# Gates of output block 1 as seven-product steps, x sums split ahead of block 0's gates, down weights and gated sums in another order

## The chip, the cores and the metric

The kernel runs on one core of a Trainium2 chip. The metric is the device time of one execution in microseconds. TensorE (PE) multiplies, VectorE (DVE), ScalarE (ACT) and GpSimd (POOL) do the elementwise work, and SyncE (SP) issues most transfers.

## The reference, cut to what matters

One layer over 512 positions with a model width of 1024, all in float32:

```
h = rms_norm(x);  proj = h @ w_in                  # conv B | conv C | conv in | q | k | v | f | gates
y_conv = (cb * causal_dwconv3(cc * cin)) @ w_out_conv
o = forgetting_attention(q, k, v, log_sigmoid(f))  # 8 heads of 64
y_attn = o @ w_out_attn
g_conv, g_attn = split(sigmoid(g_logit + b_gate))  # 2 x 1024 columns
x = x + (g_conv * y_conv + g_attn * y_attn) @ w_o
h = rms_norm(x)
a, b = split(causal_dwconv3(h @ w_up))             # 2 x 2816 columns
x = x + (silu(a) * b) @ w_down
return rms_norm(x)
```

## The kernel before

Everything is kept transposed: features on the 128 partitions, the 512 positions along a row. Every float32 operand of a product is split into a high part (rounded to the format TensorE multiplies quickly) and a low part (the rest), and a product is three passes: high x high, low x high, high x low. ScalarE makes the high part of a weight tile (wh, L275), VectorE the low part by a subtraction (wl, L279). Weights stream through `raw` tiles, fetched some tiles ahead; `stream` is the fixed list of weight tiles, and `split()` makes the parts of the next one.

Stages in order: the projections and, between them, attention; then the mixer, output block by output block (`for j in range(KB)`, eight blocks of 128 features): the two gates of block j, the tile `mix{j}` which makes yc and ya, and the merge m = gate_A * yc + gate_B * ya, split into mh and ml; then w_o; then the channel mixer in two phases of hidden pairs j = 0..11 and 12..21: up products (`up{2j}`, `up{2j+1}`), the taps of the convolution, silu and product (`glu`), and at the end of each phase the down products of that phase.

Part of the products goes by a seven-product scheme (`seven`) on 2 x 2 arrangements of blocks: two output blocks, two inner blocks, two halves of the positions. Seven products of 256 positions stand in for eight, and need sums of operands. Weight sums, called forms, are added up in DRAM by transfers (`make_forms`: SyncE's `put`, GpSimd's `add`), one group of forms per two steps. The sums of x are made on VectorE (`x_sums`), split by `x_split(q)` into xth and xtl for four quarters q. A step has a P tile (three products of a pair of blocks, 18 matmuls for two pairs) and an F tile (four products, 24 matmuls). In `passes` all high passes of a tile come first, two for each product, then the passes with the low part of the weight.

Work that has no fixed place is put in the list `later` with a due count of splits, a cost in microseconds and tags. `run_later`, called in each `split`, takes from it what fits; `flush` and `flush_only(tags)` force it out at once. Instructions that are recorded through `keep` hold the order in which the program is written; the others are placed by a scheduler after the last split.

GJ is the first block whose gates go by seven products: blocks 0 and 1 go directly before (two times 48 matmuls each, block 0's already at the end of the projections), blocks 2 to 7 by steps P0, F0, P1, F1 and so on. SUP lists the hidden pairs whose up products go by seven products: 1, 2 and 5 in phase 0, 14 and 16 in phase 1. `glu` puts sums of the gated products (ge, go) into `later`: t13 and t24 (L1253 to L1258), and their splits `hl` into gh and gl (L1262, L1263).

Of the kernel before, what the change touches and what calls it, by code (L numbers as in the profile page):

```python
# [16 lines left out]
KB = D // P  # L17
# [25 lines left out]
PHASES = ((0, 12), (12, NP))  # L43
# [8 lines left out]
    + (((1, 6),), ((1, 7), (1, 8)), ((1, 9), (1, 10))),  # L52
)

GJ = 2
GATES = tuple(((j, q), (j, q + 1)) for j in range(GJ, KB) for q in (0, 2))

PLAIN = [(m, k) for m in (6, 7) for k in range(*PHASES[1])]
# [2 lines left out]
SUP = ((1, 2, 5), (14, 16))  # L61
# [9 lines left out]
def block_kernel(ctx, tc, xT, vecs, wv, win, wmix, wo, wup, wst, wdp, outT):  # L71
# [3 lines left out]
    nc = tc.nc  # L75
# [6 lines left out]
    def keep(ins):  # L82
        return tc.keep_in_program_order(ins)
# [17 lines left out]
    def col(i):  # L101
        return vec[:, i : i + 1]
# [22 lines left out]
    stream = [(f"v{kb}", wv[kb], S + H) for kb in range(KB)]  # L125
# [7 lines left out]
    for j in range(KB):  # L133
        if j >= GJ:
            stream += step_chunks(n) + step_chunks(n + 1)
# [5 lines left out]
    ff0 = len(stream)  # L141
# [14 lines left out]
    later = []  # L156
# [7 lines left out]
        return st  # L164

    def tag_of(k):
        return "raw" if stream[k][0][0] != "F" else "rf" if k >= ff0 else "rg"

    def load(upto):
        for k in range(len(raws), min(upto, len(stream) - 1) + 1):  # L170
            nm, src, ncol = stream[k]
            tag = tag_of(k)
            if held[tag] == NRAW[tag] or tag not in pools:
                return
            held[tag] += 1
            raw = pools[tag].tile([P, D], F32, tag=tag, name=f"raw_{nm}", bufs=NRAW[tag])
            if k == 0:

                keep(nc.scalar.dma_start(raw[:, VB:ncol], src[:, VB:]))
                keep(nc.sync.dma_start(raw[:, :VB], src[:, :VB]))  # L180
            else:
                keep(nc.sync.dma_start(raw[:, :ncol], src if tag == "raw" else made[src]))
            raws.append(raw[:, :ncol])


# [2 lines left out]
    made, todo_bg = {}, []  # L188
# [58 lines left out]
    def flush_only(tags):  # L247

        while n := [n for n, w in enumerate(later) if set(w[2]) & set(tags)]:
            with after_split():  # L250
                later.pop(n[0])[3]()
# [421 lines left out]
    def run_all(fs):  # L673
        for f in fs:
            f()
# [8 lines left out]
    for t in range(NT):  # L684
        src = pa[t][:, 4 * HD : VW].unsqueeze(1).to_broadcast([P, 4, H])
# [4 lines left out]
    z, e, o = (ap.tile([n, S], F32, tag="pp", name=nm, bufs=NPP) for nm in ("fz", "fe", "fo"))  # L690
# [82 lines left out]
    k = len(parts) + 2  # L773
# [21 lines left out]
    for i in range(n + LA):  # L795
# [8 lines left out]
        if 0 <= i - LA < n:  # L804
            pr, e, qb = units[i - LA]
# [60 lines left out]
    xm = xp.tile([P, KB, S], F32, tag="x1", name="xm")  # L866
# [14 lines left out]

    def mt(name):
        mt.n += 1
        return xm[:, (mt.n + 3) % KB, :]

    mt.n = 0

    def evac_gate(idx, dst):
        def f(p):
            g = mt(f"g{idx}")  # L890
            nc.vector.tensor_mul(g, p, rb1)
            nc.scalar.activation(g, g, AF.Sigmoid, bias=col(BG + idx))
            dst.append(g)

        return f
# [10 lines left out]
    k = [c[0] for c in stream].index("mix0")  # L906
# [52 lines left out]
    for j in range(KB):  # L959
        gs = []  # L960
        for _ in range(3):
            slot()
        if j == KB - 1:
            assert mt.n == 3 * KB
            x1 = xm
            nc.gpsimd.dma_start(x1[:, :4, :], xT[:, :4, :])
        if j == 0:
            evac_gate(0, gs)(gp[0])
            evac_gate(8, gs)(gp[1])
        elif j < GJ:  # L970
            run_all(proj(20 + j, f"ga{j}", evac_gate(j, gs), acc))
            run_all(proj(28 + j, f"gb{j}", evac_gate(8 + j, gs), acc))
        else:
            if j == GJ:
                acc = ring(3, 4, 2, 7)
            seven(GATES[2 * (j - GJ) : 2 * (j - GJ) + 2], 2 * (j - GJ), {j: (0, 1, 5, 6)}, gate_form, done=gate_pair(j, gs))
        wh, wl = chunk(f"mix{j}")
        yc, ya = acc(f"yc{j}"), acc(f"ya{j}")
        for pp, hh, ll, o in ((yc, ych, ycl, 0), (ya, oth, otl, 4)):
            for k in range(4):  # L980
                ks = slice((o + k) * P, (o + k + 1) * P)
                mm3(pp, wh[:, ks], wl[:, ks], hh[:, k, :], ll[:, k, :], k == 0, k == 3)
        if j >= GJ:
            split_next()
            flush()
        a, b = gs
        nc.vector.tensor_mul(a, a, yc)
        nc.vector.tensor_mul(b, b, ya)
        nc.gpsimd.tensor_add(a, a, b)
        nc.scalar.activation(mh[:, j, :], a, AF.Copy)  # L990
        nc.vector.tensor_sub(ml[:, j, :], a, mh.bitcast(F32)[:, j, :])
# [149 lines left out]
    def up(j, ph, rb2, pu=None):  # L1141
        uu = []

        def tap(i, z):
            u = fp.tile([P, S], F32, tag="fu", name=f"fu{j}{i}", bufs=3)
            taps(u, z, CF + 3 * (2 * j + i))
            uu.append(u)

        if j in SUP[ph]:
            c = 2 * SUP[ph].index(j)  # L1150
            slot()
            seven(
                UPD[ph][c : c + 2], NU[ph] + c, {j: USETS[j]}, lambda q, g: up_form(ph, q, g), of="x",
                done=lambda i, banks, ids: merge(ph, j, banks, ids, rb2, tap, uu),
            )
            slot()
            return
        evacs = []
        for i in range(2):
            slot()  # L1160
            p = pu[i] if pu else block(f"up{2 * j + i}", x1h, x1l, True)
            if i and j + 1 == PHASES[ph][1]:
                split_next()
                if any(("e",) in w[2] for w in later):
                    flush_only((("e",),))
                    split()
            z = [None]

            def mul(i=i, p=p, z=z):
                z[0] = fp.tile([P, S], F32, tag="fz", name=f"fz{j}{i}", bufs=4)  # L1170
                nc.vector.tensor_mul(z[0], p, rb2)

            evac = [(0.7, mul), (1.4, lambda i=i, z=z: tap(i, z[0]))]
            if i:
                evac.append((0, lambda: glu(ph, j, uu)))
            if any(("e",) in w[2] for w in later):
                later.extend((0, us, (("e",), acc.last) if x == 0 else (("e",),), f) for x, (us, f) in enumerate(evac))
            else:
                for _, f in evac:
                    f()  # L1180
# [46 lines left out]
    def glu(ph, j, uu):  # L1227
        a, b = uu
        q, k = j // 2, len(parts) - 1
        g0 = place(ph, q)  # L1230
        nc.scalar.activation(a, a, AF.Silu)
        if j == NP - 1:
            nc.scalar.activation(tbl, a[: 4 * H, :1], AF.Sqrt, scale=0.0, bias=eps[: 4 * H])
        if j % 2 == 0:
            ge = glu.even = fp.tile([P, 2, 2 * P], F32, tag="ge", name=f"ge{q}", bufs=2)
            keep(nc.gpsimd.tensor_mul(ge, a.rearrange(halves_of, h=2), b.rearrange(halves_of, h=2)))  # L1236
            return
        flush_only([("q", x) for x in range(q)])
        ge = glu.even
        go = fp.tile([P, 6, 2 * P], F32, tag="gr", name=f"go{q}")  # L1240

        def mul(eng):
            return eng.tensor_mul(go[:, 0:2, :], a.rearrange(halves_of, h=2), b.rearrange(halves_of, h=2))

        if j + 1 < PHASES[ph][1]:
            keep(mul(nc.gpsimd))
        else:
            later.append((k + 3, 0.7, (("q", q),), lambda: mul(nc.vector)))
        b11, b12 = ge[:, 0, :], ge[:, 1, :]
        b21, b22, t1, t2, t3, t4 = (go[:, i, :] for i in range(6))  # L1250

        def t13():
            nc.vector.tensor_sub(t1, b11, b12)  # L1253
            nc.vector.tensor_sub(t3, b22, b12)

        def t24():
            nc.vector.scalar_tensor_tensor(t2, t1, -1.0, b22, op0=ALU.mult, op1=ALU.subtract)
            nc.vector.scalar_tensor_tensor(t4, t2, -1.0, b21, op0=ALU.mult, op1=ALU.subtract)  # L1258

        def hl(src, gs):  # L1260
            def f():
                nc.scalar.activation(gh[:, gs, :], src, AF.Copy)  # L1262
                nc.vector.tensor_sub(gl[:, gs, :], src, gh.bitcast(F32)[:, gs, :])  # L1263

            return f


        d = (2, 3, 4) if j + 1 < PHASES[ph][1] else (4, 5, 6)
        w = [(d[0], 0.85, t13), (d[0], 0.85, t24), (d[1], 0.7, hl(ge[:, : 1 + ph, :], slice(g0, g0 + 1 + NF * ph, NF)))]
        w += [(d[x > 0 and 2 or 1], 0.7, hl(go[:, x : x + 2, :], slice(g0 + 1 + x, g0 + 3 + x))) for x in (0, 4, 2)]  # L1270
        at = next((x for x, i in enumerate(later) if ("e",) in i[2]), len(later))
        later[at:at] = [(k + n, us, (("q", q),), f) for n, us, f in w]
# [264 lines left out]
```

## Time and profile before

| | |
|---|---|
| median of three runs | 694.92 us (694.84 to 695.49) |
| profiled execution | 694.18 us |
| its span | 692.4 us |
| granted TensorE clock, mean | 0.997 |
| TensorE busy | 683.1 us (99%), 5936 matmuls |
| VectorE busy | 554.2 us (80%) |
| ScalarE busy | 368.3 us (53%) |
| GpSimd busy | 190.5 us (28%) |

A row of a timeline has the start, the duration, the engine, the line, the operation, the tiles (buffer numbers left out) and, in brackets, how long the engine stood idle ahead of it and what ended that. A row of several equal instructions has their count. Times of rows are from the start of the span. In a table of windows the count behind PE's busy time is that of the matmuls that touch the window.

### The profile page before, as it was taken

Reading aid. Unit: us, or ns where it says so; the run is one execution under the profiler, and the core shown is the slowest. Engines: PE = TensorE matmul, PEld = TensorE weight load, DVE = VectorE, ACT = ScalarE, POOL = GpSimd, SP = SyncE. Lnnn points to the kernel's source line nnn. Section 1 sums busy time; section 2 is a strip of 40 time slices with the busy share of each in tenths; the row PEclk is TensorE's granted clock in tenths of the full one; section 3 lists DMA queues with packets and bytes.
Section 4 is the critical chain, followed back from the end, with each engine's and each line's share of the span. In section 5 each row is a group of like instructions: output and inputs, shape, how many; then the busy total and the mean of one; then the engine's idle time right before and its main releaser. Section 6 shows DMA issues by size and latency. Waiting matters only on the chain. (4 is left out here: it accounts for less than half of the span.)

```text
span 692.4 us, 14690 instructions
## 1 busy us (share of the span) xinstructions
PE 683.1 (99%) x5936; PEld 680.6 (98%) x5936; DVE 554.2 (80%) x858; ACT 368.3 (53%) x579; POOL 190.5 (28%) x201
## 2 busy tenths in 40 slices
PE   9999999999999999999999999999999999999996
PEld 9999999999999999999999999999999999999995
DVE  6677787877578778769879699998787899988894
ACT  5675755554554444546554555545444544545572
POOL 6134947542020201214400144340100325231000
PEclk9999999999999999999999999999999999999998
DMA  8629999552568586788998498888945996676413
GB/s 308 225 67 293 216 243 204 134 120 92 185 144 221 166 268 205 230 308 213 158 313 241 126 233 222 200 242 231 252 149 167 337 231 157 188 168 182 154 31 122
DMA packets 65012, 137.53 MB, mean 199 GB/s; under 512 B 5760, under 2 KB 30352, under 8 KB 64688
## 3 DMA queue, kind: packets, MB, share of 16 engines
q1 hardware_dynamic: 44664, 107.28, 47.2%
q0 software_dynamic: 18464, 26.03, 23.4%
q10 hardware_dynamic: 1816, 3.29, 1.3%
q8 instruction: 46, 0.75, 0.4%
q14 instruction: 22, 0.18, 0.1%
HBM read 132.31 MB, written 47.71 MB: 260 GB/s over the span
## 5 line engine op out<-in xcount | busy, mean ns | idle before, releaser
L211 POOL DMA_DIRECT2D f<-in_wst_dram x66 | 77.7, 1371 | 27.1 <-DMA f<-f 26.8
L309 PE MATMUL p_up<-x1h,wh_up 128*128 128x256 f32 x416 | 81.2, 276 | 0.0
L309 PE MATMUL p_up<-x1l,wh_up 128*128 128x256 f32 x416 | 81.0, 276 | 0.0
L309 PE MATMUL p_up<-x1h,wl_up 128*128 128x256 f32 x416 | 81.0, 276 | 0.0
L279 DVE TENSOR_TENSOR wl_F<-raw_F,wh_F 128x1024 fp32r<-128x1024 f32 (+1 forms) x42 | 55.9, 1330 | 20.0 <-ACT wh_F L275 20.0
L275 ACT ACTIVATE wh_F<-raw_F 128x1024 fp32r<-128x1024 f32 (+1 forms) x42 | 44.3, 1054 | 39.5 <-PE dn L327 28.7
L309 PEld LDWEIGHTS p_up<-x1h,wh_up 128*128 128x128 f32 x416 | 62.7, 188 | 0.0
L309 PEld LDWEIGHTS p_up<-x1l,wh_up 128*128 128x128 f32 x416 | 62.7, 188 | 0.0
L309 PEld LDWEIGHTS p_up<-x1h,wl_up 128*128 128x128 f32 x416 | 62.6, 188 | 0.0
L309 PE MATMUL p_in<-xgh,wh_in 128*128 128x256 f32 x288 | 56.8, 279 | 0.0
L309 PE MATMUL p_in<-xgh,wl_in 128*128 128x256 f32 x288 | 56.6, 278 | 0.0
L309 PE MATMUL p_in<-xgl,wh_in 128*128 128x256 f32 x288 | 56.5, 278 | 0.0
L279 DVE TENSOR_TENSOR wl_P<-raw_P,wh_P 128x768 fp32r<-128x768 f32 (+1 forms) x42 | 41.7, 992 | 14.7 <-ACT wh_P L275 8.6
L327 PE MATMUL dn<-gh,wh_F 128*128 128x256 f32 x216 | 51.2, 277 | 1.2 <-ACT wh_F L275 1.2
L275 ACT ACTIVATE wh_P<-raw_P 128x768 fp32r<-128x768 f32 (+1 forms) x42 | 35.1, 835 | 32.1 <-PE dn L327 23.2
L327 PE MATMUL dn<-gl,wh_F 128*128 128x256 f32 x216 | 51.0, 276 | 0.0
L1236 POOL TENSOR_TENSOR ge<-fu,fu 128x512 f32<-128x512 f32 x11 | 20.1, 1831 | 110.5 <-DVE fu L570 85.6
L279 DVE TENSOR_TENSOR wl_up<-raw_up,wh_up 128x1024 fp32r<-128x1024 f32 x34 | 43.8, 1288 | 7.4 <-ACT wh_up L275 7.4
L275 ACT ACTIVATE wh_up<-raw_up 128x1024 fp32r<-128x1024 f32 x34 | 35.8, 1054 | 19.4 <-PE p_up L309 9.3
L309 PEld LDWEIGHTS p_in<-xgh,wh_in 128*128 128x128 f32 x288 | 44.7, 188 | 0.7
L309 PEld LDWEIGHTS p_in<-xgl,wh_in 128*128 128x128 f32 x288 | 43.7, 188 | 0.0
L309 PEld LDWEIGHTS p_in<-xgh,wl_in 128*128 128x128 f32 x288 | 43.6, 188 | 0.0
(343 smaller groups left out, 2211.8 us busy)
## 6 DMA issues: line engine op xcount, KB each, us to landing
raw_F<-f SPq DMA_DIRECT2D x41, 512.0 KB, 5.7
raw_up<-in_wup_dram SPq DMA_DIRECT2D x34, 512.0 KB, 5.6
raw_P<-in_wst_dram SPq DMA_DIRECT2D x41, 384.0 KB, 5.4
raw_in<-in_win_dram SPq DMA_DIRECT2D x24, 512.0 KB, 3.6
f<-in_wst_dram POOLq DMA_DIRECT2D x41, 256.0 KB, 6.8
f<-in_wst_dram SPq DMA_DIRECT2D x20, 512.0 KB, 7.1
f<-in_wst_dram POOLq DMA_DIRECT2D x20, 512.0 KB, 9.1
f<-f SPq DMA_DIRECT2D x40, 256.0 KB, 6.5
```

Source lines behind the costliest of these rows:

```text
L211: return lambda: keep(nc.gpsimd.dma_start(dst, src, accum_op=ALU.add))
L275: ins = nc.scalar.activation(hi, raw, AF.Copy)
L279: ins = nc.vector.tensor_sub(lo, raw, hi.bitcast(F32))
L309: keep(nc.tensor.matmul(out[:, cs], w, x[:, cs], start=start and i == 0 and c == 0, stop=stop and i == 2 and c == len(cut) - 1,))
L327: keep(nc.tensor.matmul(out, wl if x == 1 else wh, xl if x == 2 else xh, start=opens and bk not in seen, stop=closes and bk not in left,))
L1236: keep(nc.gpsimd.tensor_mul(ge, a.rearrange(halves_of, h=2), b.rearrange(halves_of, h=2)))
```

## The change

- GJ goes from 2 to 1. The gates of block 1 become steps P0, F0, P1, F1; all later steps get numbers higher by two. The forms of one more block (one group) are made in DRAM ahead of the mixer. The raw tile of the first F step comes from the common pool, since the pool of the others is not there yet, and the tiles for merges (`mt`) start at another index.
- In the loop over blocks, for j = 0, x_split of quarters 0 and 1 is forced out ahead of block 0's gates.
- At the last up block of a phase, `split()` of the second tile of the down stage always comes, and ahead of the forced evacuations, no longer behind them and only if there are some.
- The due counts of the gated sums, d, become (4, 5, 6) at the end of a phase as before, (3, 4, 5) where the next pair goes by seven products, and (2, 3, 4) elsewhere.

```diff
-GJ = 2
+GJ = 1
...
-        return "raw" if stream[k][0][0] != "F" else "rf" if k >= ff0 else "rg"
+        return "raw" if stream[k][0][0] != "F" or stream[k][0] == "F0" else "rf" if k >= ff0 else "rg"
...
-                keep(nc.sync.dma_start(raw[:, :ncol], src if tag == "raw" else made[src]))
+                keep(nc.sync.dma_start(raw[:, :ncol], made[src] if isinstance(src, int) else src))
...
-        return xm[:, (mt.n + 3) % KB, :]
+        return xm[:, (mt.n + 1) % KB, :]
...
         if j == KB - 1:
-            assert mt.n == 3 * KB
+            assert mt.n == 3 * KB + 2
...
         if j == 0:
+            flush_only([("q", 0), ("q", 1)])
             evac_gate(0, gs)(gp[0])
             evac_gate(8, gs)(gp[1])
...
             if i and j + 1 == PHASES[ph][1]:
                 split_next()
-                if any(("e",) in w[2] for w in later):
-                    flush_only((("e",),))
-                    split()
+                split()
+                flush_only((("e",),))
...
-        d = (2, 3, 4) if j + 1 < PHASES[ph][1] else (4, 5, 6)
+        d = (4, 5, 6) if j + 1 == PHASES[ph][1] else (3, 4, 5) if j + 1 in SUP[ph] else (2, 3, 4)
```

ScalarE's rows from the end of attention into the mixer, before (wh_in21 and wh_in29 are the gate weights of block 1, xth the x sums, mh the merged block):

```order
L275 ACTIVATE wh_in21_2573<-raw_in21_2320 128x1024
L666 ACTIVATE oc31_2594<-o31_2577 64x256 x2
L669 ACTIVATE oth_96<-oc31_2594 128x256
L892 ACT_TABLE_LOAD
L892 ACTIVATE xm_2605<-xm_2605,vec_64 128x512 x2
L275 ACTIVATE wh_in29_2740<-raw_in29_2410 128x1024
L901 ACTIVATE xth_2606<-xt_103 128x1024
L990 ACTIVATE mh_2611<-xm_2605 128x512
L901 ACTIVATE xth_2606<-xt_103 128x1024
L275 ACTIVATE wh_mix1_2750<-raw_mix1_2502 128x1024
L901 ACTIVATE xth_2606<-xt_103 128x1024 x2
```

And now:

```order
L275 ACTIVATE wh_P0_2578<-raw_P0_2327 128x768
L666 ACTIVATE oc31_2599<-o31_2582 64x256 x2
L669 ACTIVATE oth_96<-oc31_2599 128x256
L901 ACTIVATE xth_2611<-xt_103 128x1024 x2
L892 ACT_TABLE_LOAD
L892 ACTIVATE xm_2610<-xm_2610,vec_64 128x512 x2
L275 ACTIVATE wh_F0_2724<-raw_F0_2417 128x1024
L275 ACTIVATE wh_P1_2754<-raw_P1_2509 128x768
L991 ACTIVATE mh_2616<-xm_2610 128x512
L901 ACTIVATE xth_2611<-xt_103 128x1024 x2
L275 ACTIVATE wh_F1_2780<-raw_F1_2716 128x1024
```

Two splits of x sums now stand ahead of the table load and block 0's sigmoids (L892), and two behind mh; where the gate weights stood there are P and F tiles, wh_F0 behind the sigmoids.

ScalarE's rows at the end of phase 0, before (F18 is the first F tile of the down stage, fu110 and fu111 the taps of the last pair, ge4 and go4 gated sums of the pair before):

```order
L566 ACTIVATE fu110_6098<-fz110_6096,vec_64 128x512
L1262 ACTIVATE gh_3988<-go4_5972 128x512 x3
L1231 ACTIVATE fu110_6098<-fu110_6098 128x512
L275 ACTIVATE wh_F18_6215<-raw_F18_5953 128x1024
L566 ACTIVATE fu111_6178<-fz111_6176,vec_64 128x512
L275 ACTIVATE wh_P19_6245<-raw_P19_6026 128x768
```

And now, where F20 and P21 are the same tiles under their new numbers:

```order
L566 ACTIVATE fu110_6113<-fz110_6111,vec_64 128x512
L1262 ACTIVATE gh_4003<-go4_5987 128x512
L1231 ACTIVATE fu110_6113<-fu110_6113 128x512
L275 ACTIVATE wh_F20_6193<-raw_F20_5968 128x1024
L1262 ACTIVATE gh_4003<-go4_5987 128x512
L566 ACTIVATE fu111_6201<-fz111_6199,vec_64 128x512
L1262 ACTIVATE gh_4003<-go4_5987 128x512
L275 ACTIVATE wh_P21_6260<-raw_P21_6041 128x768
```

The Silu (L1231) stands ahead of the F tile in both; two of the three splits of go4 moved from ahead of it to behind the F tile.

VectorE's rows between the up tiles 36 and 37, before (fz and fu are the evacuated up products and taps of pair 17, ge7 and go7 the gated sums of pairs 14 and 15):

```order
L279 TENSOR_TENSOR wl_up36_7708<-raw_up36_7472,wh_up36_7707 128x1024
L1253 TENSOR_TENSOR go7_7569<-ge7_7390 128x256
L1254 TENSOR_TENSOR go7_7569<-go7_7569,ge7_7390 128x256
L1257 SCALAR_TENSOR_TENSOR go7_7569<-go7_7569 128x256
L1171 TENSOR_TENSOR fz170_7715<-p_up34_7585,rb_n2_4668 128x512
L1258 SCALAR_TENSOR_TENSOR go7_7569<-go7_7569 128x256
L567 SCALAR_TENSOR_TENSOR fu170_7717<-fz170_7715,vec_64,fu170_7717 128x511
L570 SCALAR_TENSOR_TENSOR fu170_7717<-fz170_7715,vec_64,fu170_7717 128x510
L279 TENSOR_TENSOR wl_up37_7775<-raw_up37_7528,wh_up37_7774 128x1024
```

And now the last part of it:

```order
L1258 SCALAR_TENSOR_TENSOR go7_7584<-go7_7584 128x256
L570 SCALAR_TENSOR_TENSOR fu170_7728<-fz170_7726,vec_64,fu170_7728 128x510
L1171 TENSOR_TENSOR fz171_7732<-p_up35_7669,rb_n2_4683 128x512
L1263 TENSOR_TENSOR gl_4004<-ge7_7461,gh_4003 128x2x256
L1263 TENSOR_TENSOR gl_4004<-go7_7584,gh_4003 128x512 x2
L567 SCALAR_TENSOR_TENSOR fu171_7734<-fz171_7732,vec_64,fu171_7734 128x511
L1263 TENSOR_TENSOR gl_4004<-go7_7584,gh_4003 128x512
L570 SCALAR_TENSOR_TENSOR fu171_7734<-fz171_7732,vec_64,fu171_7734 128x510
L279 TENSOR_TENSOR wl_up37_7813<-raw_up37_7543,wh_up37_7812 128x1024
```

The seven instructions between tap L570 of fu170 and wl_up37 (fz171, four splits gl, two taps of fu171) stood behind wl_up37 before.

## The prediction

> **What bounds the kernel now.** I read the page first, then TensorE's waits, then windows along the span, then the timelines of the four places that the change touches.
>
> ```profile
> span 692.4 us, 14690 instructions
> PE 683.1 (99%) x5936; PEld 680.6 (98%) x5936; DVE 554.2 (80%) x858; ACT 368.3 (53%) x579; POOL 190.5 (28%) x201
> PE dn L327 <- ACT wh_F L275: 1.2, 2, 0.7
> PE dn L327 <- DVE wl_F L279: 0.4, 1, 0.4
> PE p_up L327 <- DVE wl_up L279: 0.2, 1, 0.2
> ```
>
> TensorE is busy for 99% of the span, and its waits on weight splits are four in number: two for the high part of an F step (wh_F, by ScalarE), one for a low part wl_F and one for wl_up (by VectorE). So time goes only with matmuls that are dropped or with a wait that comes or goes. The windows place the waits and show the clock:
>
> ```profile
> 185.00:205.00 20.00, 20.00 (x179) 20.00 (x178) 14.57 (x16) 12.05 (x14) 3.38 (x4) 1.00 0.77 186
> 460.00:480.00 20.00, 19.34 (x171) 19.15 (x170) 19.01 (x30) 11.67 (x17) 4.78 (x4) 1.00 0.91 263
> 540.00:560.00 20.00, 19.65 (x173) 19.45 (x172) 17.13 (x25) 10.38 (x14) 7.95 (x7) 1.00 1.01 287
> 600.00:620.00 20.00, 19.85 (x175) 19.65 (x174) 16.62 (x26) 9.93 (x15) 7.40 (x5) 1.00 0.60 153
> 620.00:640.00 20.00, 19.50 (x172) 19.30 (x171) 16.68 (x23) 11.55 (x16) 3.46 (x3) 1.00 0.72 183
> 187.63 0.39 PE L309 MATMUL p_ga<-xgh,wh_in 128*128 128x256 f32 x2
> 198.51 0.39 PE L309 MATMUL yc<-ych,wh_mix 128*128 128x256 f32 x2
> ```
>
> (Columns: window, its length, PE, PEld, DVE, ACT and POOL busy with instructions, PE clock, DMA share, GB/s.) An undisturbed window starts 179 matmuls; at 460, 540, 600 and 620 us it is 8, 6, 4 and 7 fewer. The last two rows hold the 96 matmuls of the direct gates of block 1: 10.88 us, 0.1133 us each. So the four waits cost some 0.91, 0.68, 0.45 and 0.79 us. The clock stayed 1.00.
>
> **A. Gates of block 1.** Removed: 96 matmuls. Added: two seven-product steps of 18 + 24, so 84. Saved: 12 x 0.1133 = **-1.36 us**. But those 10.88 us also covered the split of the x sums (xth, xtl), now needed at once. What ran there:
>
> ```profile
> 185.78 1.28 ACT L892 ACT_TABLE_LOAD   x1 [1.25 <-DVE xm L891]
> 187.07 1.34 ACT L892 ACTIVATE xm<-xm,vec 128x512 f32<-128x512 f32 x2
> 188.31 1.05 ACT L275 ACTIVATE wh_in<-raw_in 128x1024 fp32r<-128x1024 f32 x1
> 189.27 1.04 ACT L901 ACTIVATE xth<-xt 128x1024 fp32r<-128x1024 f32 x1
> 190.61 0.63 ACT L990 ACTIVATE mh<-xm 128x512 fp32r<-128x512 f32 x1 [0.29 <-POOL xm L989]
> 184.56 0.42 DVE L670 TENSOR_TENSOR otl<-oc,oth 128x256 fp32r<-128x256 f32 x1 [0.48 <-ACT oth L669]
> 187.83 0.69 DVE L987 TENSOR_TENSOR xm<-xm,yc 128x512 f32<-128x512 f32 x1 [1.52 <-ACT xm L892]
> 188.44 0.69 DVE L988 TENSOR_TENSOR xm<-xm,ya 128x512 f32<-128x512 f32 x1
> 189.39 2.26 DVE L279 TENSOR_TENSOR wl_in<-raw_in,wh_in 128x1024 fp32r<-128x1024 f32 x1 [0.27 <-ACT wh_in L275]
> 191.58 1.21 DVE L902 TENSOR_TENSOR xtl<-xt,xth 128x1024 fp32r<-128x1024 f32 x1
> 192.71 0.68 DVE L991 TENSOR_TENSOR ml<-xm,mh 128x512 fp32r<-128x512 f32 x1
> 200.06 0.96 DVE L279 TENSOR_TENSOR wl_P<-raw_P,wh_P 128x768 fp32r<-128x768 f32 x1 [1.52 <-ACT wh_P L275]
> 205.29 2.06 DVE L279 TENSOR_TENSOR wl_F<-raw_F,wh_F 128x1024 fp32r<-128x1024 f32 x1 [0.39 <-ACT wh_F L275]
> 189.27 1.30 POOL L989 TENSOR_TENSOR xm<-xm 128x512 f32<-128x512 f32 x1 [17.88 <-DVE xm L988]
> 204.98 1.29 POOL L989 TENSOR_TENSOR xm<-xm 128x512 f32<-128x512 f32 x1 [12.34 <-DVE xm L988]
> ```
>
> In the changed order ScalarE makes xth of quarters 0 and 1 first, then loads its table, does two sigmoids and only then wh_F0. xth takes the place of attention's tiles, so it starts after otl ends, at about 185.0. On the axis of before, with these durations (in the rows an instruction starts about 0.1 us ahead of the end of the one before): xth twice to 187.0, table to 188.2, sigmoids to 189.55, wh_F0 to 190.5. TensorE ends mix0 at 187.63, runs P0's 18 matmuls in 2.04 and wants wh_F0 at 189.67. So it waits about **0.9**, plus 0.1 of refill: the term of wh_F0, **1.0 us**. Before, the place of wh_F0 was taken by wh_in, which had 5 us of slack.
>
> VectorE: the two multiplies by yc and ya (0.69 each) wait for the sigmoids and end at 190.3; POOL's add follows, 190.4 to 191.7. wl_F0 begins at 190.55, beside that add. The same 1024-wide split took 2.26 us beside the add at 189.27 and 2.06 beside that at 204.98, while the 1.21 of xtl at 191.58 is the figure for that shape without it. I take 2.2: wl_F0 ends at 192.75. TensorE, 16 high products into F0 (1.81 us), wants it at 192.4: **0.35 us**. By 1.21 this term is 0. The Trainium skill, GPSIMD Engine Reference, 1. Specifications, says that GpSimd shares its SBUF interfaces with VectorE and contends with VectorE instructions that have two SBUF inputs, which the split is. By that rule the long value holds every time; without it the two long rows would be chance and the sum 0.9 lower, as wl_F0 and all that follows on VectorE would come 0.9 sooner.
>
> Then wl_P1 (0.9) to 193.65, ml (0.6) to 194.2 and only now xtl of quarters 2 and 3 (1.15 each) to 195.4 and 196.5; on ScalarE xth of these waits behind mh, which waits for POOL, and ends at 193.4 and 194.4. TensorE begins P1 at 193.7. Its sixth matmul uses xtl of quarter 2 at 194.3, so it waits **1.15**; its twelfth that of quarter 3, six matmuls on at 196.1: **0.4**. With refills of 0.1 each at the two or three waits on VectorE I have 1.0 + 0.35 + 1.15 + 0.4 + 0.2 = **+3.1 us**; bounds 2.2 (no contention) and 3.5 (table load and otl 0.3 later). From F1 on the splits are in time again: F1 gives VectorE 2.7 us for 2.1 us of work. Gates in all: **+1.75**.
>
> **B. One form group more in attention.** SyncE gets three puts more and POOL three adding DMAs.
>
> ```profile
> L211 POOL DMA_DIRECT2D f<-in_wst_dram x66 | 77.7, 1371 | 27.1 <-DMA f<-f 26.8
> 55.00:125.00 70.00, 70.00 (x598) 69.65 (x597) 56.37 (x126) 43.32 (x95) 43.74 (x53) 1.00 0.97 243
> 125.00:182.00 57.00, 57.00 (x488) 56.66 (x487) 40.09 (x91) 29.53 (x68) 20.12 (x24) 1.00 0.44 106
> ```
>
> POOL takes 3 x 1.37 = 4.1 us more, beside 43.74 of 70 busy. The DMA share is 0.97 until 125 us but 0.44 behind it, and the weights are fetched four tiles ahead while TensorE does 5.4 us per block. The group is issued after the others, so its tail falls into the half-empty stretch: **0**, from 0 to +3 should the loads slip.
>
> **C. End of phase 0.** The change names a sooner split of the first down weights. What stands in front of it:
>
> ```profile
> 466.99 0.63 ACT L1231 ACTIVATE fu<-fu 128x512 f32<-128x512 f32 x1 [0.89 <-DVE fu L570]
> 467.53 1.04 ACT L275 ACTIVATE wh_F<-raw_F 128x1024 fp32r<-128x1024 f32 x1
> 470.42 0.95 DVE L279 TENSOR_TENSOR wl_P<-raw_P,wh_P 128x768 fp32r<-128x768 f32 x1
> 472.83 0.62 PE L327 MATMUL dn<-gh,wl_P 128*128 128x256 f32 x4
> ```
>
> The wait is for wh_F, wh_F is behind the Silu L1231, and that waits for VectorE's tap L570. In the changed order the Silu still stands ahead of wh_F and the same taps ahead of it, so the 0.91 us stays: **0**. What moved are two splits of the gated sums go4, gh and gl, from ahead of wh_F to behind it. VectorE then has gl 0.6, tap 0.65, gl 0.6, tap 0.65 and wl_P (0.95) from 469.75: wl_P ends at about 473.2 to 473.3, before it was 471.37. It is wanted at 472.83: **+0.5**, from 0 to +0.7. The end of phase 1 (the 0.79 us) keeps its order: **0**.
>
> **D. Later gated sums.** The sums of a pair now start one split later around the seven-product blocks.
>
> ```profile
> 553.44 1.22 DVE L279 TENSOR_TENSOR wl_F<-raw_F,wh_F 128x1024 fp32r<-128x1024 f32 x1
> 554.72 0.38 PE L327 MATMUL dn<-x1h,wl_F 128*128 128x256 f32 x1 [0.35 <-DVE wl_F L279]
> 589.30 1.22 DVE L279 TENSOR_TENSOR wl_up<-raw_up,wh_up 128x1024 fp32r<-128x1024 f32 x1
> 592.48 0.28 PE L327 MATMUL p_up<-x1h,wh_up 128*128 128x256 f32 x1
> 593.39 0.39 PE L327 MATMUL p_up<-x1h,wl_up 128*128 128x256 f32 x2
> ```
>
> At 554 us wl_F moves ahead of one sum L1258 and one gl, but stays behind sums that wait for POOL's product. I get its end 0.5 us earlier than the 554.66 of these rows, just when it is wanted: **-0.45**, from -0.65 to 0. At 590 us the reverse: wl_up37, ended at 590.52, now stands behind fz171, four gl splits and both taps of fu171, which were behind it. Seven instructions of about 0.62 us, 4.3 us, bring it to 594.8 at the most, to 594.2 if L1258 ahead of them is not held up by GpSimd's work as before; wanted at 593.39, so with refill 0.9 to 1.5: **+1.1**, and down to +0.4 where the scheduler's gaps close up further. For this wl_up40 at 609 has fewer splits in front of it, and its wait goes: **-0.45**. The sums at q = 0, 5 and 10 stay in time: 0.
>
> Sum: -1.36 + 3.1 + 0.5 - 0.45 + 1.1 - 0.45 = **+2.45 us** on the profiled 694.18, so 696.6. The median of the runs is 694.92, 0.74 over it; the median forecast is **697.4**.
>
> **The rivals.** (1) The gate waits are no larger than the products saved: no POOL contention (-0.9), xth and table 0.3 earlier (-0.5), wl_up37 at its low end (-0.7). The sum is then +0.35, 695.3. Against it: the rows of 2.26 and 2.06; chance 0.15. (2) The change does what its words say: all splits in time at the gates (-1.36), the wait at 460 gone (-0.9), wl_F's and wl_up's gone (-1.1), nothing new: 691.6. Against it: wh_F0 is behind a table load and two sigmoids that cannot start sooner. Chance 0.06. (3) The further form group displaces loads in the 0.97 stretch, each load late by more than its four-tile cover: 3 us above the forecast, 700.4. TensorE never waited there with six groups; chance 0.05. (4) The waits, four or five within 10 us, pull the clock down: some 20 matmuls after them at half pace are 2.3 us more, 699.7. Against it: 1.00 in windows with 0.91 and 0.79 us of wait; chance 0.03. The Trainium skill, TensorE: Matmul & The Clock Gate, Why this matters for your kernels, asks for gaps under about 3 us; its section A second HAM failure mode: psum-queue depth-cycling holds frequent short idles to be enough. The four windows agree with the first and cannot try the second. The forecast keeps 0.71.
>
> **How the numbers follow.** What a measurement of this kernel can tell from no change is about 0.2%, 1.39 us: same is 693.53 to 696.31. Faster is rival 2 with a little from rival 1's tail, 0.07. Same takes rival 1, 0.15, and a small part of the forecast's low end, 0.02. Slower: the rest, 0.76. The range goes from 695.2 (rival 1) to 699.3 (gate bound 3.5, phase end 0.7, wl_up37 1.5, no gain at 554: 697.4 + 0.4 + 0.2 + 0.4 + 0.45 = 698.85, and half of the way to rival 4).
>
> **What would show it.** In the profile after: TensorE's waits gain a wait for wh_F near 189.7 of about 0.9 us and one or two for xtl near 194.3; 12 matmuls fewer in all (5924); ScalarE's wh_F at the end of phase 0 still right after a Silu, with a wait of unchanged size; a wait for wl_up near 593 and none at 554 and 609. The prediction is wrong if the window from 185 to 205 shows under 10 matmuls missing, if the wait at the end of phase 0 is gone, or if TensorE waits during attention.

## The result, and the profile after

The changed kernel takes 699.84 us (median of five runs, 699.24 to 699.96), the kernel before 694.89 us beside it: 4.95 us more, a ratio of 1.0070 with a 95% interval of 1.0057 to 1.0082. The forecast was 697.4, from 695.2 to 699.3. The side was right; the size was half of what came, and the time lies 0.5 us above the range.

The page and TensorE's waits of the changed kernel:

```profile
span 698.2 us, 14694 instructions
PE 684.1 (98%) x5924; PEld 680.9 (98%) x5924; DVE 558.9 (80%) x865; ACT 370.8 (53%) x582; POOL 191.7 (27%) x204
PE dn L327 <- ACT wh_F L275: 1.7, 2, 0.9
PE p_up L327 <- DVE wl_up L279: 1.4, 1, 1.4
PE dn L327 <- DVE gl L1263: 1.3, 1, 1.3
PE dn L327 <- DVE xtl L902: 1.0, 2, 0.8
PE tp L641 <- DVE ptl L645: 0.5, 1, 0.5
```

The 12 matmuls are gone (5924). One of the two waits for wh_F is a new one, at the gates, and one of the old ones has gone. The waits for gl and for ptl were not forecast; the one for ptl is in attention, where the prediction had named any wait as a sign that it is wrong. The windows hold them (same columns as before; an undisturbed window has 179 matmuls):

```profile
185.00:205.00 20.00, 18.07 (x151) 17.27 (x150) 17.04 (x21) 12.46 (x15) 3.35 (x3) 1.00 0.82 219
463.00:483.00 20.00, 18.93 (x163) 18.53 (x162) 17.41 (x26) 10.40 (x15) 4.78 (x4) 1.00 0.87 240
545.00:565.00 20.00, 20.00 (x179) 20.00 (x178) 16.04 (x25) 9.37 (x14) 6.48 (x7) 1.00 1.01 255
592.00:612.00 20.00, 18.58 (x164) 18.39 (x163) 19.57 (x29) 10.47 (x15) 6.97 (x4) 1.00 0.58 158
640.00:660.00 20.00, 18.65 (x163) 18.38 (x162) 14.89 (x23) 9.32 (x13) 0.00 (x0) 1.00 0.54 159
```

28 matmuls are missing in the first, 16, 0, 15 and 16 in the others; the clock stays 1.00 in all. In the timelines the gates look like this (ScalarE, VectorE, GpSimd, then TensorE):

```profile
186.21 2.01 ACT L901 ACTIVATE xth<-xt 128x1024 fp32r<-128x1024 f32 x2 [0.49 <-DVE otl L670]
188.24 1.28 ACT L892 ACT_TABLE_LOAD   x1
189.54 1.34 ACT L892 ACTIVATE xm<-xm,vec 128x512 f32<-128x512 f32 x2
190.79 1.04 ACT L275 ACTIVATE wh_F<-raw_F 128x1024 fp32r<-128x1024 f32 x1
191.86 2.26 DVE L279 TENSOR_TENSOR wl_F<-raw_F,wh_F 128x1024 fp32r<-128x1024 f32 x1 [0.26 <-ACT wh_F L275]
195.51 2.35 DVE L902 TENSOR_TENSOR xtl<-xt,xth 128x1024 fp32r<-128x1024 f32 x2
191.74 1.29 POOL L990 TENSOR_TENSOR xm<-xm 128x512 f32<-128x512 f32 x1 [19.11 <-DVE xm L989]
191.88 0.38 PE L327 MATMUL dn<-xgh,wh_F 128*128 128x256 f32 x1 [0.81 <-ACT wh_F L275]
196.78 0.39 PE L327 MATMUL dn<-xtl,wh_P 128*128 128x256 f32 x1 [0.81 <-DVE xtl L902]
197.91 0.39 PE L327 MATMUL dn<-xtl,wh_P 128*128 128x256 f32 x1 [0.16 <-DVE xtl L902]
```

ScalarE goes through xth, table, sigmoids and wh_F without a gap, and TensorE waits for the last of them; VectorE reaches the xtl of quarters 2 and 3 only after the long wl_F, wl_P and ml. This is the picture that the prediction drew, 1.2 us later on the axis.

Starts of TensorE's stages, subtracted, give the length of each in each profiled execution. Differences from the kernel before, in us (the stages before attention differ by up to 0.5 among executions whatever the kernel, once by 1.8, and are left out; the stages not listed differ by under 0.15, but for up 30 and 31 where a line says so):

| kernel | attention | mixer | down, phase 0 | up 28, 29 (pair 14) | up 34 to 43 | down, phase 1 |
|---|---|---|---|---|---|---|
| length before | 129.58 | 111.58 | 58.06 | 10.17 | 54.92 | 36.68 |
| changed | +0.75 | +1.83 | +0.85 | -0.65 | +1.19 | +1.19 |
| e1 gates alone | +0.69 | +1.96 | +0.28 | 0.00 | -0.08 | +0.44 |
| e2 due counts alone | +0.02 | 0.00 | +0.04 | -0.49 | +1.01 | -0.65 |
| e3 end split alone | +0.02 | 0.00 | +0.62 | 0.00 | +0.23 | +2.35 |
| e4 form group alone | +0.71 | 0.00 | +0.03 | 0.00 | +0.01 | +0.13 |
| e5 changed, add on VectorE | +0.69 | +1.32 | +0.88 | -0.65 | +1.17 | +1.23 |
| e6 gates behind mix1 | +0.85 | +0.63 | +0.45 | 0.00 | -0.01 | +0.11 |
| e7 Silu behind F | +0.02 | 0.00 | -0.94 | +0.08 | +0.21 | +1.17 |
| e8 group by SyncE | +0.02 | 0.00 | +0.01 | +0.01 | -0.01 | +0.02 |
| e9 e7, counts one lower | +0.07 | 0.00 | -0.94 | +0.01 | +0.27 | -0.75 |
| e10 e9, pair 13 later | +0.07 | 0.00 | -0.94 | -0.56 | +0.22 | -0.85 |

For the changed kernel these sum to 5.16 us. Each row is one execution of the kernel; its sum can differ from the difference of the medians, most in e1 (3.4 against 2.4 us). A wait of TensorE that the text gives with two decimals is the distance of two starts of products less the usual 0.113; the next product comes another 0.11 late (the refill). TensorE's wait lists give the idle time alone, which is shorter.

### The profile page after: what moved, and what is told of

Read it like the earlier page. It is cut to its first block, busy times and chain, and to the rows that moved or that the text cites. A ratio compares the mean times of both kernels' runs of the same rounds, so it can differ in the third digit from the quotient of the medians.

```text
span 698.2 us, 14694 instructions
## 1 busy us (share of the span) xinstructions
PE 684.1 (98%) x5924; PEld 680.9 (98%) x5924; DVE 558.9 (80%) x865; ACT 370.8 (53%) x582; POOL 191.7 (27%) x204
## 5 line engine op out<-in xcount | busy, mean ns | idle before, releaser
L211 POOL DMA_DIRECT2D f<-in_wst_dram x69 | 79.8, 1337 | 27.7 <-DMA f<-f 27.6
L279 DVE TENSOR_TENSOR wl_F<-raw_F,wh_F 128x1024 fp32r<-128x1024 f32 (+1 forms) x44 | 59.6, 1353 | 21.4 <-ACT wh_F L275 21.4
L275 ACT ACTIVATE wh_F<-raw_F 128x1024 fp32r<-128x1024 f32 (+1 forms) x44 | 46.4, 1054 | 38.3 <-PE dn L327 28.1
L275 ACT ACTIVATE wh_P<-raw_P 128x768 fp32r<-128x768 f32 (+1 forms) x44 | 36.8, 836 | 41.6 <-PE dn L327 24.1
L279 DVE TENSOR_TENSOR wl_up<-raw_up,wh_up 128x1024 fp32r<-128x1024 f32 x34 | 45.8, 1347 | 5.6 <-ACT wh_up L275 5.3
L1236 POOL TENSOR_TENSOR ge<-fu,fu 128x512 f32<-128x512 f32 x11 | 17.8, 1619 | 107.6 <-DVE fu L570 85.7
```

The costliest lines, as they stand in the source:

```text
L211: return lambda: keep(nc.gpsimd.dma_start(dst, src, accum_op=ALU.add))
L275: ins = nc.scalar.activation(hi, raw, AF.Copy)
L279: ins = nc.vector.tensor_sub(lo, raw, hi.bitcast(F32))
```

## The experiments

**e1, the gates alone.** The changed kernel with these two pieces as before:

```diff
-                split()
-                flush_only((("e",),))
+                if any(("e",) in w[2] for w in later):
+                    flush_only((("e",),))
+                    split()
...
-        d = (4, 5, 6) if j + 1 == PHASES[ph][1] else (3, 4, 5) if j + 1 in SUP[ph] else (2, 3, 4)
+        d = (2, 3, 4) if j + 1 < PHASES[ph][1] else (4, 5, 6)
```

> The kernel before with the gates part of the change alone (GJ = 1, its raw tile, merge tiles and the two early x splits); the due counts of the gated sums and the order at the end of a phase stay as before. Theory (from the two traces, place by place): the gates cost 1.84 us in all (four waits of 3.2 us less 12 matmuls of 1.36) and the form group more in attention 0.7 us by GpSimd's queue, so +2.5 us. Rival: the 0.7 us in attention is only how that one execution went, so +1.8. Second rival: the gates' waits depend on nothing else but hold less in other executions, so under +1.

697.74 us against 695.38, ratio 1.0034 (1.0022 to 1.0045), some 2.4 us. Attention +0.69 and mixer +1.96 again, so both belong to the gates and the first was no accident of one execution. The down stage of phase 0 is 0.28 longer here, without any edit there: its wait for wh_F is longer (1.09 against 0.82; also in e6). The 0.28 begins at the Silu of the pair before, here in the kernel before and then in e1:

```profile
456.56 0.63 ACT L1231 ACTIVATE fu<-fu 128x512 f32<-128x512 f32 x1 [2.70 <-DVE fu L570]
459.96 0.63 ACT L1232 ACTIVATE fu<-fu 128x512 f32<-128x512 f32 x1 [2.98 <-DVE fu L570]
```

The tap it waits for starts at 455.72 and 458.84 and takes 0.75 in both, so the Silu comes 0.09 us behind the tap before and 0.37 in e1, and VectorE keeps these 0.28 up to the taps of the last pair, and so its Silu and wh_F have them. Why the Silu itself starts late the trace does not show. No run takes the early splits of the x sums out of the gates part, so their share in it is not known.

**e2, the due counts alone**, in the kernel before:

```diff
-        d = (2, 3, 4) if j + 1 < PHASES[ph][1] else (4, 5, 6)
+        d = (4, 5, 6) if j + 1 == PHASES[ph][1] else (3, 4, 5) if j + 1 in SUP[ph] else (2, 3, 4)
```

> The kernel before with the due counts (3, 4, 5) ahead of seven-product pairs alone. Theory: wl_F at 554 us in time -0.65, wl_up37 late +1.7, wl_up40 in time -0.5, and the wait at the end of phase 1 (0.77) goes, as VectorE and ScalarE catch up while TensorE waits for wl_up37: -0.2 us in all. Rival: the wait at the end of phase 1 has nothing to do with it and stays: +0.6 us.

695.02 against 695.38, ratio 0.9992 (0.9982 to 1.0001). TensorE's waits:

```profile
PE p_up L327 <- DVE wl_up L279: 1.2, 1, 1.2
PE warm L115 <- DVE ones L107: 1.1, 1, 1.1
PE dn L327 <- ACT wh_F L275: 0.7, 1, 0.7
```

The wait for wl_F has gone, wl_up37 is late by 1.2, and of the two waits for wh_F one is left: the one at the end of phase 1 has gone (down, phase 1: -0.65), though nothing was edited there. TensorE's wait for wl_up37 lets VectorE catch up, so that the Silu at the end of the phase comes sooner against TensorE: 1.86 us ahead of the first down product (630.43 and 632.29), before it was 0.54 (630.54 and 631.08). A wait that is bought here pays off a wait behind it; the rival, +0.6, lies outside the interval. 0.33 of the gain is lost again in up 30 and 31.

**e3, the end split alone**, in the kernel before (the reverse of the first piece of e1's diff).

> The kernel before with the unconditional split ahead of the forced evacuations at the last up block alone. Theory: glu of the last pair then counts one split more, so all its sums come due one split later; end of phase 0 +0.85 us, end of phase 1 a wait for the last gl split of 1.0 to 1.7 us, the wait for wh_F at both ends unchanged: +1.9 to +2.6 us. Rival: the late gl comes from the due counts in the other edit, and this one alone costs only the end of phase 0: +0.85 or less.

698.34 against 695.38, ratio 1.0041 (1.0028 to 1.0054), 3.0 us: the dearest of the three parts, and more than the 2.6 expected at most. Waits:

```profile
PE dn L327 <- DVE gl L1262: 1.4, 1, 1.4
PE dn L327 <- ACT wh_F L275: 1.3, 2, 0.7
PE dn L327 <- DVE wl_P L279: 0.3, 1, 0.3
```

Both waits for wh_F are still there, so the first down weights are not split sooner; a wait for wl_P (the forecast 0.5) and one for gl are new. The last is the larger. The waits make some 1.9 of the 2.35 us by which the last down stage is longer; the rest is a pace of 0.118 us a product in stretches behind the waits, for which the trace shows no cause. `glu` takes its due counts from the number of splits done so far (`k = len(parts) - 1`); with the second split ahead of the evacuation that number is one higher, and all the last pair's sums come one split later. In the changed kernel the last gl stands behind wl_F at the time when TensorE asks for it (VectorE, then TensorE):

```profile
650.89 1.22 DVE L279 TENSOR_TENSOR wl_F<-raw_F,wh_F 128x1024 fp32r<-128x1024 f32 x1
652.02 0.68 DVE L1263 TENSOR_TENSOR gl<-go,gh 128x512 fp32r<-128x512 f32 x1
651.02 0.38 PE L327 MATMUL dn<-gh,wh_P 128*128 128x256 f32 x1
652.76 0.39 PE L327 MATMUL dn<-gl,wh_P 128*128 128x256 f32 x1 [1.35 <-DVE gl L1263]
```

The three parts add up to some 2.4 - 0.4 + 3.0 = 5.0 us, the 4.95 of the whole. That they meet so closely is luck: the intervals are 0.6 to 0.9 us to either side, and in the last down stage the parts give 0.44 - 0.65 + 2.35 = 2.14 where the whole has 1.19.

**e4, a form group more that nobody reads**, in the kernel before:

```diff
+        if key == "gate":
+            m, g = 2 * P, g + 1
+            f = dr.tile([P, 2, 4 * m], F32, tag="fx", name="fx")
...
+            ops = (put(f0, x0), add(f0, x1), put(f1, f[:, :, :m]), add(f1, x1[:, :, m:]), put(f2, f1), add(f2, x2))
```

> The kernel before with a seventh group of gate forms made in attention that nobody reads (three puts by SyncE and three adding transfers by GpSimd more, at the slots where the change has them); nothing else differs. Theory: GpSimd's adding transfers stand ahead of its scaling of the attention weights, which come later to TensorE: +0.7 us, as a wait of TensorE near 122 us. Rival: 0 within 0.3, the wait of the profiled execution was chance.

695.45 against 695.38, ratio 1.0003 (0.9991 to 1.0016): 0.7 us more lies inside that interval, and so does nothing; the runs don't tell. The trace does: attention +0.71, with TensorE's wait for ptl (0.5) as in the changed kernel, its only wait in attention. The way to it, before and then in e4 (its line numbers are 8 higher, and its attention starts 0.36 us later, at 52.90 for 52.54):

```profile
110.97 2.25 POOL L597 TENSOR_TENSOR y<-y,u 128x512 f32<-128x512 f32 x1
113.25 0.63 ACT L598 ACTIVATE ych<-y 128x512 fp32r<-128x512 f32 x1 [2.47 <-POOL y L597]
113.91 0.69 DVE L599 TENSOR_TENSOR ycl<-y,ych 128x512 fp32r<-128x512 f32 x1 [2.50 <-ACT ych L598]
121.07 0.68 DVE L645 TENSOR_TENSOR ptl<-tp,pth 128x512 fp32r<-128x512 f32 x1
```

```profile
109.33 1.44 POOL L211 DMA_DIRECT2D fx<-in_wst_dram  x1
112.14 2.25 POOL L605 TENSOR_TENSOR y<-y,u 128x512 f32<-128x512 f32 x1
114.43 0.63 ACT L606 ACTIVATE ych<-y 128x512 fp32r<-128x512 f32 x1 [3.26 <-POOL y L605]
115.10 0.69 DVE L607 TENSOR_TENSOR ycl<-y,ych 128x512 fp32r<-128x512 f32 x1 [3.49 <-ACT ych L606]
122.26 0.69 DVE L653 TENSOR_TENSOR ptl<-tp,pth 128x512 fp32r<-128x512 f32 x1
123.09 0.30 PE L649 MATMUL tp<-ident,pp 128*128 128x128 f32 x1 [0.53 <-DVE ptl L653]
```

The adding transfer of fx went ahead of attention's work on GpSimd. The product y of the convolution, which GpSimd makes behind it, comes 1.17 us later on the axis, 0.81 without the later start of attention. ScalarE (ych) and VectorE (ycl) stand idle for y in both kernels, so they pass the delay on: ptl is 0.83 later against the start of attention, and TensorE waits for it. The expectation named the scaling of the attention weights; the trace leads to y. kb, which brings two rows that the scores need, was put behind fx and a scaling as well (107.79, now 111.00), but no wait of TensorE for it shows.

**e8, the same bytes by SyncE.** e4 with six plain copies, none from GpSimd:

```diff
-            ops = (put(f0, x0), add(f0, x1), put(f1, f[:, :, :m]), add(f1, x1[:, :, m:]), put(f2, f1), add(f2, x2))
+            ops = [put(d, s) for d, s in zip(fs, (x0, x1, x0[:, :, :m], x1[:, :, m:], x1[:, :, :m], x2))]
```

> The kernel before with transfers of the bytes of a seventh form group in attention, but all six issued by SyncE as plain copies to places that nobody reads, none by GpSimd. Theory: the wait of 0.7 us near 122 us was GpSimd's queue (an adding transfer ahead of a step of attention), so it is gone and attention lasts as before, within 0.1 us. Rival: it was the traffic or SyncE's queue, and attention is again 0.7 us longer.

694.73 against 695.07, ratio 0.9996 (0.9987 to 1.0005). Attention is +0.02 and the wait for ptl is gone; y starts here at 111.26, with attention 0.27 later than before, so at its old place. So it was GpSimd's queue, and neither SyncE's nor the traffic of plain copies. An adding transfer can be told from a copy only together with GpSimd here: no run has GpSimd issue copies in its place.

**e5, block 0's merge add on VectorE**, in the changed kernel:

```diff
-        nc.gpsimd.tensor_add(a, a, b)
+        (nc.gpsimd if j else nc.vector).tensor_add(a, a, b)
```

> The changed kernel with one edit: block 0's merge add runs on VectorE instead of GpSimd. Theory: wl_F0 took 2.26 us because GpSimd's add ran beside it; without it 1.21, and the add itself is 0.6 on VectorE, so VectorE has 0.45 us less to do before the x sums of quarters 2 and 3; their wait falls from about 1.0 to 0.5, the stage of the mixer is 0.4 to 0.6 us shorter than in the changed kernel. Rival: wl_F0 stays near 2.2 us (it is long for another reason) and the stage grows by 0.6.

698.88 against 695.07, ratio 1.0055 (1.0041 to 1.0068). The mixer is 0.52 us shorter than in the changed kernel:

```profile
191.35 0.69 DVE L990 TENSOR_TENSOR xm<-xm 128x512 f32<-128x512 f32 x1
191.96 1.22 DVE L279 TENSOR_TENSOR wl_F<-raw_F,wh_F 128x1024 fp32r<-128x1024 f32 x1
```

wl_F0 fell from 2.26 to 1.22 as soon as no GpSimd add ran beside it. VectorE pays 0.69 for the add itself, so half of the gain is left. Here the Trainium skill's rule (GPSIMD Engine Reference, 1. Specifications), that GpSimd contends with VectorE instructions with two SBUF inputs, and the trace agree; the 1.04 us is this case's own number.

**e6, mix1 ahead of block 1's gates.** e1 with another order of the stream, so that TensorE has 48 products between mix0 and the first step. Block 2's gates also get other banks, and the split of F2, the first F step of block 2, is held behind the sums of block 1's gates; the main part:

```diff
+        if j > GJ:
+            gates()
         wh, wl = chunk(f"mix{j}")
...
+        if j == GJ:
+            gates()
+            flush_only((0, 1, 5, 6))
+            split()
```

> Gates of block 1 by seven products, but with mix1's 48 products put ahead of them, so that 5.4 us of products lie between mix0 and the first step; block 2's gates then use banks 3, 5, 4, 0 and follow block 1's gates at once; due counts and phase ends as before. Theory: the gates' waits come only from the lost cover, so the four waits of 3.2 us are gone and the mixer is 0.4 to 0.9 us shorter than in the kernel before (12 products less, a wait of 0.5 to 0.9 for a bank at the first step of block 2); with 0.7 in attention and up to 0.7 at the later places that the gates alone showed, the kernel is within 0.7 us of the kernel before. Rival: the waits stay, as VectorE and ScalarE have too much to do there whatever the order; then +2 us or more.

696.63 against 695.07, ratio 1.0021 (1.0012 to 1.0030). The four waits at block 1's gates are gone, so they came from the cover, as said. But the mixer is still 0.63 longer than before, where I expected it 0.4 to 0.9 shorter, and the kernel 1.6 us slower than before, where I expected at most 0.7. Block 2's first step now follows at once and waits for a bank of the accumulators (0.53), and behind mix2 the first F step of block 3 waits for wh_F (0.68) and wl_F (0.24). TensorE's rows:

```profile
PE dn L339 <- ACT wh_F L287: 2.0, 3, 0.9
PE dn L339 <- DVE xm L939: 0.4, 1, 0.4
204.37 0.38 PE L339 MATMUL dn<-xth,wh_P 128*128 128x256 f32 x1 [0.36 <-DVE xm L939]
221.81 0.39 PE L339 MATMUL dn<-xgh,wh_F 128*128 128x256 f32 x1 [0.51 <-ACT wh_F L287]
```

(Of the three waits for wh_F the other two are those at the phase ends.) The cover was moved, not made: in the kernel before it stood between the end of attention and the first step and cost 12 products.

**e7, the Silu of the last pair behind the first F split**, in the kernel before:

```diff
+            elif i and j + 1 == PHASES[ph][1]:
+                split()
+                with after_split():
+                    for _, f in evac:
+                        f()
```

> The kernel before with one edit: the evacuation of the last pair of each phase, its taps and its Silu come behind the split of the first F tile (the split is taken one step sooner, and they are placed behind it). Theory: the Silu ahead of wh_F is the cause of the waits of 0.93 and 0.78 us at the two phase ends; they go. But the sums of the last pair count one split more, as in the changed kernel: a wait for the last gl of up to 1.6 us at the end of phase 1 remains, so -1.7 to +0.5 us in all, with both waits for wh_F gone. Rival: the waits are set by the buffer of the weight tile or the transfer of it, and stay.

695.81 against 695.07, ratio 1.0012 (1.0003 to 1.0021), 0.7 us where +0.5 was the most expected. No wait for wh_F is left:

```profile
PE dn L327 <- DVE gl L1268: 1.4, 1, 1.4
PE p_up L327 <- DVE wl_up L279: 0.4, 1, 0.4
PE dn L327 <- DVE wl_F L279: 0.4, 1, 0.4
466.50 1.07 ACT L275 ACTIVATE wh_F<-raw_F 128x1024 fp32r<-128x1024 f32 x1 [0.96 <-ACT gh L1267]
467.99 0.62 ACT L1236 ACTIVATE fu<-fu 128x512 f32<-128x512 f32 x1
```

So what stood ahead of wh_F was the cause of both: the Silu with the taps it waits for, and at the end of phase 1 also the table load behind it, which the edit moved along. ScalarE's rows there before (wh_F follows at 632.69):

```profile
630.54 0.63 ACT L1231 ACTIVATE fu<-fu 128x512 f32<-128x512 f32 x1 [2.15 <-DVE fu L570]
631.19 1.28 ACT L1233 ACT_TABLE_LOAD   x1
```

The down stage of phase 0 is 0.94 shorter; that of phase 1 gains its wait for wh_F and loses the late gl, which the extra split brings here as in e3.

**e9, the counts one lower**, in e7:

```diff
-        q, k = j // 2, len(parts) - 1
+        q, k = j // 2, len(parts) - 1 - (j + 1 == PHASES[ph][1])
```

> The kernel of e7 (Silu of the last pair behind the first F split) with one edit: the due counts of the last pair's sums start one split lower, so that they come at the splits where they came before. Theory: the late gl at the end of phase 1 (1.6 us) is due to the one split more that glu counts, and goes; with the waits for wh_F gone too, STEPS of phase 0 are 0.9 and of phase 1 0.6 to 0.8 us shorter than before: -1.4 to -1.7 us. Rival: the late gl follows from the later taps of the last pair, whatever the counts; then 0 to +1.

693.53 against 695.08, ratio 0.9977 (0.9968 to 0.9986). The late gl is gone (down, phase 1: -0.75): the count was its cause.

**e10, and the later sums for one pair only**, in e9:

```diff
-        d = (2, 3, 4) if j + 1 < PHASES[ph][1] else (4, 5, 6)
+        d = (4, 5, 6) if j + 1 == PHASES[ph][1] else (3, 4, 5) if j == 13 else (2, 3, 4)
```

> The kernel of e9 with the later due counts (3, 4, 5) of the change for the one pair ahead of hidden pair 14, and not ahead of pair 16. Theory: the wait of 0.63 us for wl_F near 554 us goes and the late wl_up37 does not come: 0.2 to 0.6 us less than e9. Rival: the sums that are pushed back there make another wait in the next up blocks, and nothing is won.

692.86 against 695.08, ratio 0.9968 (0.9956 to 0.9981): 2.2 us faster than before and some 7 us faster than the changed kernel, with the gates of block 1 direct. All that the list of TensorE's waits still has:

```profile
PE warm L115 <- DVE ones L107: 1.1, 1, 1.1
PE p_up L327 <- DVE wl_up L279: 0.4, 1, 0.4
```

By the stages, e10 wins 0.56 at pair 14 over the kernel before and gives 0.31 back in up 30 and 31. Its median is 0.7 below that of e9, the intervals overlap.

## Why the prediction was wrong in size

The forecast failed at two terms that it put at nothing: the form group in attention (B) and the end of phase 1 ("keeps its order: 0", "stay in time: 0"). Together they cost 1.9 us, and its range held nothing for either.

- **Gates, +1.75 forecast, +1.83 measured.** The steps held one by one: a wait of 0.9 for wh_F0 (0.97), wl_F0 at 2.2 (2.26) and a wait of 0.35 for it (0.31), xtl of quarter 2 (1.15 forecast, 0.98) and of quarter 3 (0.4, 0.33). e5 shows the contention term, e6 the lost cover.
- **Attention, 0 forecast, +0.75.** The first step that failed: I weighed the form group by the DMA share and the loads, and put its tail into the half-empty stretch. TensorE waited for no load in attention. I did count GpSimd's 4.1 us, but held them against a mean (43.74 of 70 us busy) and not against what stands behind the transfers in GpSimd's queue: the product y, for which ScalarE and VectorE are already idle before. It comes 0.81 later in e4, and not in e8.
- **End of phase 0, +0.5 forecast, +0.85.** That the split does not come sooner, and why, was right (e3, e7). The wait for wl_P is 0.31 plus 0.11 of refill, near the forecast. Another 0.28 come with the gates (e1), from a Silu that starts late; why it does, and the last 0.15, stay open.
- **Down stage of phase 1, 0 forecast, +1.19.** The second step that failed: the sentence "The sums at q = 0, 5 and 10 stay in time: 0" was wrong for the last pair. I read the due counts, which stay (4, 5, 6) there, and not the number of splits that `glu` adds them to, which the moved split raises by one. Two things are hidden in the 1.19: a late gl of 1.62 (1.77 with what is lost around it; e3, e9) and the old wait for wh_F (0.77 with refill), which goes since TensorE waits at wl_up37 ahead of it (e2). A wait for wh_P near the stage's end, longer by 0.15, makes up most of the rest. "keeps its order: 0" was wrong too: the sums came one split later, and the Silu and wh_F, whose order did stay, met TensorE at another time.
- **Later sums, -0.45 + 1.1 - 0.45 forecast.** Right in all three signs: -0.65 at pair 14; 1.58 at wl_up37, 1.69 with refill, where VectorE's L1253 took 0.92 beside GpSimd's product and the split ended at 598.21, which is 594.9 on the axis of before (3.3 earlier), just behind the 594.8 that I had as the latest; wl_up40's wait gone.

The sum of the terms missed by 2.7 us, of which 1.2 stood in the last down stage, 0.75 in attention and 0.5 in wl_up37. The first rival (fewer gate waits), the second (all splits in time) and the one of the clock did not come; the third named the place in attention, but for another reason and a quarter of the price. That the side came out right rests on the gates, whose steps held.

## What to carry to other kernels

Products that are saved on the bounding engine were also the cover of what ran beside them: take them away only with a schedule for what they covered. Moving a split ahead wins nothing if the instruction that holds the engine is still ahead of it, and it makes all work later whose due time is counted in splits done; look for both. A transfer that an engine has to issue costs that engine's queue as well, so a new one is weighed against the elementwise work behind it, not only against bandwidth; and a wait in one place can take one away behind it, so waits are not summed as if each stood alone.

## What the runs showed of the hardware that was not expected

GpSimd's adding transfers hold up its own elementwise work: with one more ahead of it, the product y came 0.81 us later against the start of attention (e4) and attention lasted 0.71 longer, while the same bytes in copies from SyncE moved attention by 0.02 (e8). A 128x1024 subtraction on VectorE took 1.04 us more beside a 128x512 add of GpSimd (2.26 against 1.22, e5). The clock did not move, as the forecast had it: four waits of 0.3 to 1.0 us within 8 us left the granted clock at 1.00.
